# Gate steps, silu and first Down splits in other places around the end of the Up stage

## The chip, the cores and the metric

The kernel runs on one core of one Trainium2 chip. The metric is the device time of one execution in microseconds (us), lower is better. Inside the core, TensorE (PE) multiplies, ScalarE (ACT) and VectorE (DVE) do elementwise work, GpSimd (POOL) does elementwise work and starts some transfers, and SyncE (SP) starts most transfers. Each of them runs its own list of instructions strictly in order, and waits at an instruction until what it needs is there.

## The reference

One decoder layer: a conditioned norm, a mixer (linear recurrence and sparse attention side by side), a gated residual, and then the part that matters here, a gated MLP with a causal convolution of width 3 and a gate vector `gt2` that is one of six products of the condition `c`:

```python
mod = cs @ w_ada[l] + b_ada[l]
sh1, sc1, gt1, sh2, sc2, gt2 = [m[:, None, :] for m in jnp.split(mod, 6, axis=-1)]
...
h2 = rmsnorm(x, norm2_g[l]) * (1.0 + sc2) + sh2
u = causal_dwconv(h2 @ w_up[l], conv_w[l], conv_b[l])
a, v = jnp.split(u, 2, axis=-1)
x = x + gt2 * ((jax.nn.silu(a) * v) @ w_down[l])
```

There are 512 tokens, a model width of 1024 and an inner width of 2816, all in float32.

## The kernel before

Every large product is made of three: each float32 operand is split into a high part (a CAST on ACT, L150) and a low part (a TENSOR_TENSOR subtraction on DVE, L151), and `mm3` (L154 to L156) multiplies high by high, high by low and low by high into one PSUM bank. So a weight tile must have passed ACT for its first matmul and DVE for the first one that reads its low part. `split` and `mm3` are helpers, so almost all of this work carries lines 150 to 156, and is told apart by tile names.

The stages from the middle of the kernel on are:

- **Up, eight early tiles** (loop at L2062), then **seven groups** (`x_group`, L1985). A group is a block product of Up for one pair of weight columns: PE works through x-products and v-products, while ACT and DVE split the next weights and make the convolution taps of results (`taps`, L1767: one ACT and two DVE instructions, from PSUM into an SBUF tile `y`). `held` is a list of three functions that the group before left for this one to run (taps, silu and gate products).
- **Up, eight tail tiles** (loop at L2085). They are called T0 to T7 below; T0 and T1 are the two halves of one load, and so on. Each is 24 matmuls of 128x512 (`u<-...`), from weights that are split on the way (`piece`, `parts`). Behind the matmuls of a tile the loop runs `up_post` (L1802) for the tile two before it: `post_taps`, then `post_gate`. `gate` (L1775) is a silu on ACT (L1778) for even tiles, and for odd tiles three or four products and sums on POOL (L1785 to L1794).
- **Down**: steps u = 0, 1, ... of 24 matmuls of 128x512 each (`dn<-...`), called D0, D1, ... below. In D0 to D10 each step adds three matmuls to each of eight PSUM accumulators in turn. `dn_load(u)` fetches weights, `dn_split(u)` splits them (two casts on ACT, two subtractions on DVE), and `a_split` splits the left operand (`as<-ga`). `ahead_of(u)` runs `dn_load(u + 3)` and `dn_split(u + 1)` ahead of the matmuls of step u. All eight PSUM banks are in use: the accumulators of D0 take the banks that the taps of T0 to T7 leave, the last of them T7's.

Beside this, `gt2` is made by sixteen **gate steps** (`last_add`, L1507): an ACT instruction scales a fetched row block `aw` of `w_ada` (L1510), POOL adds it to `gt2` (L1511), and SP starts the fetch of the next block (`last_fetch`, L1499). The first eight steps make the left half of `gt2`, the other eight the right half. Then `last_split` splits a half into `rhi` and `rlo`, and `last_spread` (L1522) sums it over the partitions with two matmuls and copies the result back with ACT (L1526).

`EARLY` (L54) says for how many Down steps the left operand is split already in the tail of Up; `put_by` (L1809) does one such split for each `beside()` there, and also stores tiles that are needed much later to DRAM (`later<-gb`). `back` (L1831) fetches them again. Temporary 128x512 tiles (`y`, `aw`, `rhi`, `rlo`) share a ring of eight buffers, so a fetch into such a tile waits for the last reader of the tile that lay there.

The order of the work is the order in which the code is written: no scheduler moves instructions.

Of the kernel before, what the change touches and what calls it, by code (L numbers as in the profile page):

```python
# [50 lines left out]
EPOS = 1  # L51
VLAG = 1
ADL = 1
EARLY = 6  # L54
PRE = 4
NU = NFF // 2
XS = (2, 3, 4, 5, 6, 7, 8)
# [52 lines left out]
def hybrid_layer_kernel(ctx: ExitStack, tc: tile.TileContext, d: dict, out: bass.AP, dbg=None):  # L110
# [21 lines left out]
    def PS(s="ps"):  # L132
        return psum.tile([P, 512], F32, tag="b", name=nm(s))
# [1373 lines left out]
    def last_add(s, res):  # L1507
        r, q, k = last_raw.pop(0)
        acc = res[:, q * 512:(q + 1) * 512]
        sc.activation(r, r, AF.Copy, scale=cs[:, k:k + 1])  # L1510
        gp.tensor_tensor(acc, acc, r, ALU.add)  # L1511
        last_fetch(s)

    last_parts = []
# [4 lines left out]
        split(hi, lo, res[:, q * 512:(q + 1) * 512])  # L1519
        last_parts.extend((hi, lo))  # L1520

    def last_spread(res, q):  # L1522
        ps = PS()
        for n in range(2):
            pe.matmul(ps, onesr, last_parts.pop(0), start=(n == 0), stop=(n == 1))
        sc.copy(res[:, q * 512:(q + 1) * 512], ps)  # L1526


    x1 = []
# [272 lines left out]
    def up_post(st):  # L1802
        post_taps(st)
        post_gate(st)
# [4 lines left out]
    def put_by(now):  # L1809
        for j in sorted(full_at, key=full_at.get):  # L1810
            if now >= full_at[j] + 4:
                del full_at[j]
                sp.dma_start(later[j], PB.pop(j)[:, 0:3])
                if place[j] < EARLY:
                    unsplit.append(j)
        if unsplit and XT < now:
            j = unsplit.pop(0)
            a_split(place[j], PA.pop(j))

# [139 lines left out]
    def prepare_plain(n):  # L1959
        p = prep[n]  # L1960
        p["b"] = [G([2, 4, P], F32R, s="wg") for _ in range(2)]
        split(*p["b"], p["raw"][:, 0].rearrange("p (b k) f -> p b k f", b=2))
# [22 lines left out]
    def x_group(n):  # L1985
# [13 lines left out]
        sc.copy(m1, X)  # L1999
        v_mm(V[0], p["v1"], range(4))  # L2000
        held.pop(0)()
        if n > 4:
            last_add(5, gt2)
        beside()
        x_mm(X, half(p["t12"], 1), ops[2], False)
        x_mm(Z, half(p["t12"], 0), ops[1])
# [16 lines left out]
        ve.tensor_tensor(R, n5, X, ALU.subtract)  # L2023
        if more:
            prepare_plain(n + 1)
        v_mm(V[1], p["v2"], range(4))
        taps(uf[1], 0, j + NU)
        last_add(5, gt2)
# [1 line left out]
        v_mm(V[1], p["v2"], range(4, KT))  # L2030
        if more:
            prepare_rest(n + 1)
        x_mm(X, p["x4"], h22, False)
        if more:
            prepare_other(n + 1)
        else:
            piece()
            last_fetch(5)
        del prep[n]

        def first():
# [43 lines left out]
    for st in range(NH, nst):  # L2085
        beside()
        if st == nst - 3:
            dn_load(0)
        elif st == nst - 1:
            dn_load(1)  # L2090
        up_mm(st, full)
        if held:
            for f in held:
                f()
            held.clear()
        elif st > NH + 1:
            up_post(st - 2)
        for _ in range(2 if st == NH else st < NH + 6):
            last_add(5, gt2)
        if st in (NH + 2, nst - 1):  # L2100
            last_spread(gt2, st == nst - 1)
        if st in (NH + 1, nst - 2):
            last_split(gt2, st == nst - 2)
    dn_split(0)
    up_post(nst - 2)
    up_post(nst - 1)
    dn_load(2)
    n = 2 * NU

    def ahead_of(u):  # L2110
        if u + 3 < n:
            dn_load(u + 3)
        if u == 0:
            put_by(tick[0] + 9)
            assert not full_at and not unsplit
        if u + 1 < n:
            dn_split(u + 1)

    for u in range(NU - 1):
        ahead_of(u)  # L2120
        if 0 <= u - EARLY + 1 < PRE:
            back(PAIRS[u - EARLY + 1])
        if 0 <= u - EARLY < PRE:
            a_split(u - EARLY + NU, PB.pop(PAIRS[u - EARLY]))
        for m in TERMS[0]:
            for i in range(2):
                dn_mm(u, m, i)
# [118 lines left out]
```

## Time and profile before

| what | value |
|---|---|
| time, median of 3 runs | 681.27 us (681.12 to 681.4) |
| time of the profiled execution | 680.94 us |
| its span, first to last instruction | 679.2 us |
| mean granted TensorE clock | 0.999 of full speed |
| busy time of PE / DVE / ACT / POOL | 662.6 / 549.6 / 382.7 / 179.4 us |
| the groups, by the PE's records | about 370 to 516.4 us |
| T0 to T7 | 516.4 to 562.7 us |
| D0 onward | from 565.0 us |

A time in a row of the profile is counted from the start of the span. A row of the timeline gives start, duration, engine, line, operation and tiles, and in brackets how long the engine had been idle before and which engine and line ended that. The waits view sums such idle times by who waited for whom. Matmuls overlap each other: one of 128x512 is recorded as 0.39 us, but in steady work the next one starts 0.23 us after it. A gap between starts therefore shows a loss better than the idle time does.

### The profile page before, as it was taken

The page shows a single profiled execution, that of the slowest core. Times are in us where ns is not written, and L with a number is a line of the kernel's source. Part 1 is how long each engine was busy: PE and PEld are TensorE (multiplying, and loading weights), DVE is VectorE, ACT ScalarE, POOL GpSimd, SP SyncE. Part 2 cuts the span into 40 slices and gives each one's busy share as a digit, 9 for nine tenths or more (in the row PEclk, how much of TensorE's full clock was granted, in tenths as well). Part 3 has the DMA queues.
Part 4 walks back from the last instruction along what each step waited for, and adds up shares of the span by engine and source line. Part 5 has one row for each costly group of instructions (what it writes and reads, how often), then busy time and mean ns, then how long its engine had stood idle before and what let it go on. Part 6 is the DMA issues. An engine that isn't in the chain of part 4 may idle for free. (4 is left out here: it accounts for less than half of the span.)

```text
span 679.2 us, 11713 instructions
## 1 busy us (share of the span) xinstructions
PE 662.6 (98%) x4400; PEld 557.9 (82%) x4400; DVE 549.6 (81%) x1038; ACT 382.7 (56%) x713; POOL 179.4 (26%) x172
## 2 busy tenths in 40 slices
PE   8999999999999999999999999999999997999996
PEld 4778898788888888888988989889898785888885
DVE  5788988979899878688778778898876877676997
ACT  5756437747677777246465536455465646464451
POOL 1006121000010100100456444465555874100000
PEclk9999999999999999999999999999999999999999
DMA  9936363566213316036668699999987782896672
GB/s 332 412 143 208 95 213 124 190 216 219 80 48 114 106 58 249 10 125 192 195 165 250 164 282 223 242 264 305 240 235 209 204 289 61 304 362 218 216 280 93
DMA packets 101885, 134.67 MB, mean 198 GB/s; under 512 B 6507, under 2 KB 67780, under 8 KB 101829
## 3 DMA queue, kind: packets, MB, share of 16 engines
q1 hardware_dynamic: 96885, 121.28, 52.8%
q0 software_dynamic: 4512, 11.54, 9.9%
q10 hardware_dynamic: 432, 1.12, 0.4%
q8 instruction: 34, 0.56, 0.3%
q14 instruction: 22, 0.18, 0.1%
HBM read 125.39 MB, written 31.60 MB: 231 GB/s over the span
## 5 line engine op out<-in xcount | busy, mean ns | idle before, releaser
L151 DVE TENSOR_TENSOR wlo<-raw,whi 128x1024 fp32r<-128x1024 f32 (+1 forms) x53 | 69.5, 1312 | 37.1 <-ACT whi L150 37.1
L156 PE MATMUL u<-h2h,wlo 128*128 128x512 f32 (+1 forms) x248 | 93.5, 377 | 1.5 <-DVE wlo L151 1.5
L154 PE MATMUL u<-h2h,whi 128*128 128x512 f32 (+1 forms) x248 | 93.5, 377 | 0.0
L155 PE MATMUL u<-h2l,whi 128*128 128x512 f32 (+1 forms) x248 | 93.4, 377 | 0.0
L150 ACT CAST whi<-raw 128x1024 fp32r<-128x1024 f32 (+1 forms) x53 | 53.9, 1019 | 18.2 <-PE u L155 7.9
L156 PEld LDWEIGHTS u<-h2h,wlo 128*128 128x128 f32 x248 | 46.7, 188 | 11.2 <-DVE wlo L151 2.7
L154 PEld LDWEIGHTS u<-h2h,whi 128*128 128x128 f32 x248 | 46.8, 189 | 7.7
L155 PEld LDWEIGHTS u<-h2l,whi 128*128 128x128 f32 x248 | 46.8, 189 | 7.6
L150 ACT CAST whi<-wd 128x1024 fp32r<-128x1024 f32 x20 | 21.1, 1055 | 39.6 <-PE dn L156 32.0
L372 POOL TENSOR_TENSOR hrs<-hrs,mhalf 128x4 f32<-128x4 f32 (+2 forms) x16 | 18.6, 1172 | 90.7 <-DVE hrs L371 88.6
L1087 ACT ACTIVATE pt<-pt,mx 128x128 f32<-128x128 f32 (+3 forms) x64 | 35.9, 564 | 9.2 <-DVE mx L1071 8.2
L154 PE MATMUL pT<-hT,whi 128*128 128x512 f32 x96 | 38.4, 400 | 0.0
L151 DVE TENSOR_TENSOR wlo<-wd,whi 128x1024 fp32r<-128x1024 f32 x20 | 25.5, 1276 | 15.2 <-ACT whi L150 15.2
L155 PE MATMUL pT<-hT,whi 128*128 128x512 f32 x96 | 37.5, 391 | 0.0
L156 PE MATMUL pT<-hT,wlo 128*128 128x512 f32 x96 | 37.5, 391 | 0.0
L154 PE MATMUL dn<-whi,as 128*128 128x512 f32 x88 | 34.4, 391 | 1.6 <-ACT whi L150 1.6
L155 PE MATMUL dn<-wlo,as 128*128 128x512 f32 x88 | 34.6, 393 | 1.3 <-DVE wlo L151 1.1
L156 PE MATMUL dn<-whi,as 128*128 128x512 f32 x88 | 34.3, 389 | 0.0
L1127 ACT COPY pT<-F 128x512 f32<-128x512 f32 (+2 forms) x52 | 25.8, 499 | 13.2 <-PE F L1120 13.2
L1071 DVE CUSTOM_DVE_ANT_0 pt<-S,cmask 128x128 f32<-128x128 f32 (+3 forms) x64 | 29.7, 486 | 2.1 <-PE S L1067 2.0
L1792 POOL TENSOR_TENSOR ga<-y,y 128x256 f32<-128x256 f32 x11 | 13.7, 1243 | 60.5 <-ACT y L1778 49.2
L1511 POOL TENSOR_TENSOR gt<-gt,aw 128x512 f32<-128x512 f32 x16 | 23.8, 1486 | 21.8 <-ACT aw L1510 21.5
(409 smaller groups left out, 2022.7 us busy)
## 6 DMA issues: line engine op xcount, KB each, us to landing
raw<-in_w_up SPq DMA_DIRECT2D x44, 512.0 KB, 6.4
aw<-in_w_ada SPq DMA_DIRECT2D x24, 512.0 KB, 3.9
ada<-in_ada_first SPq DMA_DIRECT2D x16, 512.0 KB, 8.1
raw<-in_w_in SPq DMA_DIRECT2D x7, 1024.0 KB, 5.0
wt<-in_w_down POOLq DMA_DIRECT2D x11, 512.0 KB, 9.0
wd<-in_w_down SPq DMA_DIRECT2D x11, 512.0 KB, 3.8
wt<-in_w_down SPq DMA_DIRECT2D x10, 512.0 KB, 9.7
wt<-in_w_down POOLq DMA_DIRECT2D x5, 1024.0 KB, 10.2
```

Source lines behind the costliest of these rows:

```text
L150: sc.copy(hi, src)
L151: (eng or ve).tensor_tensor(lo, src, f32(hi), ALU.subtract)
L154: pe.matmul(o, ah, bh, start=start, stop=False, skip_group_check=True)
L155: pe.matmul(o, ah, bl, start=False, stop=False, skip_group_check=True)
L156: pe.matmul(o, al, bh, start=False, stop=stop, skip_group_check=True)
L372: gp.tensor_tensor(o, o, mhalf[:, 0:n], ALU.pow)
L1071: ve.tensor_tensor_reduce(pt[:, e * W:(e + 1) * W], ps[:, e * W:(e + 1) * W], cmask[:, 512 - W:512], -1.0, 1e30, ALU.add, ALU.min, mx[:, e ...
L1087: sc.activation(pt[:, sl], pt[:, sl], AF.Exp, bias=mx[:, e:e + 1], scale=-1.0, accum_out=su[:, h % 2, e:e + 1])
L1127: sc.copy(pT, ps[:, 0:n * P])
L1511: gp.tensor_tensor(acc, acc, r, ALU.add)
L1792: gp.tensor_tensor(a[:, 0], g[:, 0:256], y[:, 0:256], ALU.mult)
```

## The change

- All sixteen gate steps run inside the groups. Before, the first five groups had one each, the last two groups two each, and the tail seven. Now every group has two, and the last has two more.
- `last_spread` is cut in two: the two matmuls stand ahead of T2 and ahead of T4, the copy (`last_out`) follows behind the tile's other work. Before, matmuls and copy came together behind T2 and behind T7. The splits of the two halves are made behind T1 and T3.
- In the tail, the gate of a tile runs one tile later than its taps (`post_gate(st - 3)`, `post_taps(st - 2)`); the gates of the last two tiles run in D0.
- Four left operands are split early, not six, and one for every other tile. `back` and the splits of the second phase that hang on `EARLY` come two steps earlier.
- `dn_split(1)` stands ahead of the taps of T7, and `put_by` for the rest in D1 and not in D0.
- T0's weights go to tiles of the large pool (`wg`) in place of the pair `whi`, `wlo`.

```diff
-EARLY = 6
+EARLY = 4
@@ last_spread
-    def last_spread(res, q):
-        ps = PS()
+    last_ps = []
+
+    def last_spread():
+        last_ps.append(PS())
         for n in range(2):
-            pe.matmul(ps, onesr, last_parts.pop(0), start=(n == 0), stop=(n == 1))
-        sc.copy(res[:, q * 512:(q + 1) * 512], ps)
+            pe.matmul(last_ps[0], onesr, last_parts.pop(0), start=(n == 0), stop=(n == 1))
+
+    def last_out(res, q):
+        sc.copy(res[:, q * 512:(q + 1) * 512], last_ps.pop())
@@ put_by
-        if unsplit and XT < now:
+        if unsplit and XT < now and (now - XT) % 2:
@@ x_group
         held.pop(0)()
-        if n > 4:
-            last_add(5, gt2)
+        last_add(5, gt2)
         beside()
...
         if more:
             prepare_plain(n + 1)
+        else:
+            last_add(5, gt2)
         v_mm(V[1], p["v2"], range(4))
         taps(uf[1], 0, j + NU)
         last_add(5, gt2)
...
         if more:
             prepare_rest(n + 1)
+        else:
+            last_add(5, gt2)
         x_mm(X, p["x4"], h22, False)
         if more:
             prepare_other(n + 1)
         else:
-            piece()
-            last_fetch(5)
+            piece(True)
@@ the tail
+        if st in (NH + 2, NH + 4):
+            last_spread()
         up_mm(st, full)
...
         elif st > NH + 1:
-            up_post(st - 2)
-        for _ in range(2 if st == NH else st < NH + 6):
-            last_add(5, gt2)
-        if st in (NH + 2, nst - 1):
-            last_spread(gt2, st == nst - 1)
-        if st in (NH + 1, nst - 2):
-            last_split(gt2, st == nst - 2)
+            if st > NH + 2:
+                post_gate(st - 3)
+            post_taps(st - 2)
+        if st in (NH + 1, NH + 3):
+            last_split(gt2, st == NH + 3)
+        if st in (NH + 2, NH + 4):
+            last_out(gt2, st == NH + 4)
     dn_split(0)
-    up_post(nst - 2)
-    up_post(nst - 1)
+    post_gate(nst - 3)
+    post_taps(nst - 2)
     dn_load(2)
+    dn_split(1)
+    post_taps(nst - 1)
@@ ahead_of
-        if u == 0:
+        if u == 1:
             put_by(tick[0] + 9)
             assert not full_at and not unsplit
-        if u + 1 < n:
+        if 0 < u < n - 1:
             dn_split(u + 1)
 
     for u in range(NU - 1):
         ahead_of(u)
+        if u == 0:
+            post_gate(nst - 2)
+            post_gate(nst - 1)
```

The next lists show what that does to the instruction lists. A row has line, operation, written tile, read tiles and size; lines of the changed kernel are a few higher (L1774 for L1770, L1782 for L1778, L1530 for L1526).

The first place is ACT's list at the end of the last group, from the taps of the group's result (`y<-uf`) to the casts of T0's and T1's weights. Before:

```order
L1770 ACTIVATE y_5957<-uf_5796,cv 128x512
L1510 ACTIVATE aw_5853<-aw_5853,cs 128x512
L150 CAST whi_5994<-raw_5786 128x1024
L150 CAST whi_6001<-raw_5786 128x1024
L1770 ACTIVATE y_6030<-u_5798,cv 128x512
L1778 ACTIVATE y_5957<-y_5957 128x512
```

The same place on ACT in the changed kernel:

```order
L1510 ACTIVATE aw_5873<-aw_5873,cs 128x512
L1774 ACTIVATE y_5981<-uf_5816,cv 128x512
L1510 ACTIVATE aw_5967<-aw_5967,cs 128x512
L1510 ACTIVATE aw_5987<-aw_5987,cs 128x512
L150 CAST wg_6020<-raw_5806 128x1024
L150 CAST whi_6025<-raw_5806 128x1024
```

Three gate steps (`aw`) stand there and not one, two of them between the taps and the cast for T0, which now writes `wg`.

The second place is ACT's list in the tail around the cast of T4's weights (`whi_6159` before, `whi_6162` now). Before, behind the silu of T0:

```order
L1778 ACTIVATE y_6137<-y_6137 128x512
L1510 ACTIVATE aw_6055<-aw_6055,cs 128x512
L1526 COPY gt_3810<-ps_6146 128x512
L150 CAST as_6151<-ga_4798 128x1024
L150 CAST whi_6159<-raw_6065 128x1024
```

In the changed kernel, from the cast of T3's weights (`whi_6120`) on:

```order
L150 CAST whi_6120<-raw_6017 128x1024
L1774 ACTIVATE y_6148<-u_6024,cv 128x512
L1530 COPY gt_3810<-ps_6116 128x512
L150 CAST as_6154<-ga_4490 128x1024
L150 CAST whi_6162<-raw_6081 128x1024
L1782 ACTIVATE y_6148<-y_6148 128x512
```

The silu of T0 went from ahead of T4's cast to behind it, and no gate step is left there.

The third place is the start of Down, first on ACT: `whi_6374` and `wg_6378` before, `whi_6361` and `wg_6365` now, are D0's weights, the next such pair D1's. Before:

```order
L150 CAST rhi_6327<-gt_3810 128x512
L1770 ACTIVATE y_6361<-u_6250,cv 128x512
L1526 COPY gt_3810<-ps_6370 128x512
L150 CAST whi_6374<-raw_6246 128x1024
L150 CAST wg_6378<-raw_6246 128x1024
L1770 ACTIVATE y_6382<-u_6293,cv 128x512
L1778 ACTIVATE y_6382<-y_6382 128x512
L1770 ACTIVATE y_6387<-u_6336,cv 128x512
L150 CAST whi_6407<-raw_6332 128x1024
```

On ACT in the changed kernel, at the same place:

```order
L1774 ACTIVATE y_6357<-u_6251,cv 128x512
L150 CAST whi_6361<-raw_6247 128x1024
L150 CAST wg_6365<-raw_6247 128x1024
L1774 ACTIVATE y_6374<-u_6285,cv 128x512
L150 CAST whi_6383<-raw_6327 128x1024
L150 CAST wg_6387<-raw_6327 128x1024
L1774 ACTIVATE y_6391<-u_6331,cv 128x512
L1782 ACTIVATE y_6374<-y_6374 128x512
```

The split and the copy of `gt2` are gone from here, and D1's casts stand ahead of the taps of T7 (`y_6387` before, `y_6391` now). DVE's list in the changed kernel, from the low part of D0's second pair of weights on, shows the same:

```order
L151 TENSOR_TENSOR wg_6366<-raw_6247,wg_6365 128x1024
L1775 SCALAR_TENSOR_TENSOR y_6374<-u_6285,cv,y_6374 128x511
L1776 SCALAR_TENSOR_TENSOR y_6374<-u_6285,cv,y_6374 128x510
L151 TENSOR_TENSOR wlo_6384<-raw_6327,whi_6383 128x1024
L151 TENSOR_TENSOR wg_6388<-raw_6327,wg_6387 128x1024
L1775 SCALAR_TENSOR_TENSOR y_6391<-u_6331,cv,y_6391 128x511
L1776 SCALAR_TENSOR_TENSOR y_6391<-u_6331,cv,y_6391 128x510
```

Before, the two low parts of D1 stood behind the taps of T7; now the taps of T7 stand behind them.

## The prediction

> **What bounds the kernel now.** The page puts PE at 98% of the span, and the granted clock at full speed, so time can only go where PE stands still. I first asked the waits view for PE from 340 us on, where Up and Down lie:
>
> ```profile
> PE dn L154 <- ACT whi L150: 1.6, 1, 1.6
> PE u L156 <- DVE wlo L151: 1.5, 2, 1.2
> PE dn L155 <- DVE wlo L151: 1.1, 1, 1.1
> PE dn L154 <- DVE y L1772: 0.8, 1, 0.8
> ```
>
> There are five waits in all, for split weights (`whi`, `wlo`) and once for taps (`y`). The timeline of PE then shows where they are:
>
> ```profile
> 516.61 0.40 PE L155 MATMUL u<-h2l,whi 128*128 128x512 f32 x1
> 517.32 0.50 PE L156 MATMUL u<-h2h,wlo 128*128 128x512 f32 x1 [0.32 <-DVE wlo L151]
> 517.65 0.39 PE L154 MATMUL u<-h2h,whi 128*128 128x512 f32 x1
> ...
> 528.11 0.39 PE L155 MATMUL u<-h2l,whi 128*128 128x512 f32 x1
> 528.47 0.50 PE L156 MATMUL u<-h2h,wlo 128*128 128x512 f32 x1
> ...
> 539.74 0.39 PE L155 MATMUL u<-h2l,whi 128*128 128x512 f32 x1
> 541.29 0.50 PE L156 MATMUL u<-h2h,wlo 128*128 128x512 f32 x1 [1.16 <-DVE wlo L151]
> ...
> 562.75 0.39 PE L1525 MATMUL ps<-rhi,onesr 128*128 128x512 f32 x1
> 562.98 0.40 PE L1525 MATMUL ps<-rlo,onesr 128*128 128x512 f32 x1
> 564.99 0.49 PE L154 MATMUL dn<-whi,as 128*128 128x512 f32 x1 [1.62 <-ACT whi L150]
> 566.62 0.50 PE L155 MATMUL dn<-wlo,as 128*128 128x512 f32 x1 [1.14 <-DVE wlo L151]
> ...
> 571.06 0.39 PE L156 MATMUL dn<-wg,as 128*128 128x512 f32 x1
> 572.26 0.47 PE L154 MATMUL dn<-wg,as 128*128 128x512 f32 x1 [0.81 <-DVE y L1772]
> ```
>
> In steady work starts lie 0.23 us apart (562.75 to 562.98). What is over that is lost: 0.48 in T0, 0.13 in T2, 1.32 in T4, 1.78 and 1.40 at the first two matmuls of D0, and 0.97 at D0's last accumulator, in sum 6.1 us. Behind a wait the next start comes 0.33 and not 0.23 later (517.32 to 517.65), five times 0.1, so **6.6 us** are lost. From 380 us to T0, and from D1 to the last product, no other wait of note shows. This is the most that the change can win here, since it leaves PE's work as it is.
>
> Why PE waits there is read from ACT and DVE:
>
> ```profile
> 534.46 0.63 ACT L1778 ACTIVATE y<-y 128x512 f32<-128x512 f32 x1 [4.88 <-DVE y L1772]
> ...
> 537.03 1.05 ACT L150 CAST whi<-raw 128x1024 fp32r<-128x1024 f32 x1
> ...
> 558.28 0.63 ACT L1778 ACTIVATE y<-y 128x512 f32<-128x512 f32 x1 [4.26 <-DVE y L1772]
> ...
> 563.41 0.58 ACT L1526 COPY gt<-ps 128x512 f32<-128x512 f32 x1 [1.85 <-PE ps L1525]
> 563.89 1.05 ACT L150 CAST whi<-raw 128x1024 fp32r<-128x1024 f32 x1
> 564.84 1.05 ACT L150 CAST wg<-raw 128x1024 fp32r<-128x1024 f32 x1
> 565.79 0.78 ACT L1770 ACTIVATE y<-u,cv 128x512 f32<-128x512 f32 x1
> ...
> 569.78 0.76 ACT L1770 ACTIVATE y<-u,cv 128x512 f32<-128x512 f32 x1
> ```
>
> ```profile
> 538.92 2.31 DVE L151 TENSOR_TENSOR wlo<-raw,whi 128x1024 fp32r<-128x1024 f32 x1
> ...
> 564.97 1.60 DVE L151 TENSOR_TENSOR wlo<-raw,whi 128x1024 fp32r<-128x1024 f32 x1 [1.84 <-ACT whi L150]
> 566.49 1.21 DVE L151 TENSOR_TENSOR wg<-raw,wg 128x1024 fp32r<-128x1024 f32 x1
> 567.63 0.74 DVE L1771 SCALAR_TENSOR_TENSOR y<-u,cv,y 128x511 f32<-128x511 f32 x1
> 568.40 0.75 DVE L1772 SCALAR_TENSOR_TENSOR y<-u,cv,y 128x510 f32<-128x510 f32 x1
> ```
>
> ACT stands at a silu for 4.88 us, then does a gate step, a copy and an early split, and only at 537.03 casts T4's weights; DVE's part ends at 541.23, and PE goes on at 541.29. At Down it stands at the copy of `gt2` until PE has made the second spread (563.0), and only then casts D0's weights, which nobody needed to wait for.
>
> **The change part by part.** PE's list has the same matmuls. Without a wait it would run T0 and T1 from 516.38 (0.23 ahead of 516.61), 24 times 0.227 = 5.45 us each, to 527.29, the first spread (0.46) and T2 and T3 to 538.66, the second spread and T4 to T7 to 560.93. I set each engine's new list against these times.
>
> *D0's first matmuls (1.78 + 1.40 and a restart, 3.3 us).* The copy waits for a spread that now stands ahead of T4, 22 us earlier. ACT casts D0's weights when the buffers of T6 come free, at 555.5; with the 1.05 of a cast, and 0.95 from cast to cast, DVE has both low parts by about 559 (1.05 + 1.2 + 1.2, from the rows at 563.89 to 566.49), even 560.5 if each takes 0.4 to 1.1 more. PE needs the first at 561.2. The term goes to nothing; what is late next there is the transfer of D0's weights, whose place in SP's list hardly moves.
>
> *T4 (1.4 us).* Its cast no longer stands behind the silu. It waits for T2's end (533.2), the cast and the subtraction end by 535.5, by 536.7 if DVE takes 2.31 again, and PE wants it at 539.5. Goes to nothing. T3, T5, T6 and T7 are laid out alike: two tiles of buffer, so 5.45 us for 2.3 us of splitting. The two spreads need `rlo` at 527.5 and 538.9; on ACT and DVE it ends near 526.8 and 537.8, with less than a microsecond to spare. I keep 0.2 us for that.
>
> *D0's last accumulator (0.97 and a restart).* This stays. T7's taps, at 569.78 on ACT before, now follow D1's two casts and two subtractions. Before, from ACT's cast at 563.89 through two subtractions to the end of the next taps at 569.15 was 5.26 us, with 0.38 of delay in it (1.60 against 1.21). The same run begins at T7's end, 560.93, and PE needs the bank 21 matmuls later, 4.77 us. So 0.3 to 0.7 is lost, with a restart, and up to 2.4 us if DVE comes late out of the tail: it has fourteen instructions, some 12.7 us, between T5's end (550.0) plus a cast and the bank. I take **0.6**.
>
> *T0 (0.6 us).* T0's cast is free of PE now, but two gate steps stand ahead of it. These rows are of ACT's and SP's timeline, of the tile view of `aw` from 470 to 565 us, and of the transfer engines from 502 to 516 us (forty slices, busy tenths):
>
> ```profile
> 512.13 0.71 ACT L1510 ACTIVATE aw<-aw,cs 128x512 f32<-128x512 f32 x1
> 507.96 0.34 SPq L1499 DMA_DIRECT2D aw<-in_w_ada  x1
> DMA to landing us min/median/max: 5.3/7.9/9.4
> DMA  9998999999999999973387610028789999999999
> ```
>
> The step at 512.13 stays, a second follows, then cast and subtraction: 512.13 + 2 x 0.71 + 1.05 + 1.22 = 515.8, ahead of 516.84, when PE reads the low part. So T0 gains its 0.6 if the last fetch is there. This is a new wait: behind the gate step stand the casts of T0 and T1 and the taps. The buffer of that fetch comes free with the same POOL product as that of the SP row, so it is asked for at 507.96, and must land within 4.9 us, by 512.84. Fetches of `aw` landed in 5.3 to 9.4, but the transfer engines stand empty near 510.5, so the fetch that before was asked for at the very same moment had landed in 2.5. I take it as in time.
>
> *The groups.* Five of them get one more ACT step of 0.71 and one more addition on POOL of 1.3. The last two groups had both already, at the same place, and PE lost nothing there. One row of the waits from 380 to 515 us, and one of the windows (busy time of PE, PE's loads, DVE, ACT and POOL in a group's 21 us):
>
> ```profile
> ACT u L2007 <- PE uf L156: 15.5, 6, 2.8
> 435.00:456.00 21.00, 21.00 (x132) 18.95 (x131) 17.86 (x22) 10.70 (x16) 11.25 (x10) 1.00 0.95 256
> ```
>
> ACT waits 2.6 us a group for PE right behind that place, so the step lies in idle time; DVE is busy for 17.86 of the 21 us of a group. Cost zero; less than nothing it can't be, since PE loses nothing there; for more, see the rivals. The seven steps that leave the tail (ACT 0.71, POOL 1.3 each) free those engines where PE waited. Moving the splits of D4 and D5 into Down costs DVE 1.2 us in a step of 5.45 that has 2.5 to 3.7 us of work, which PE covers. `put_by` in D1 lets the loads of D4 go ahead of a store that waits for POOL: also no cost.
>
> Sum: 6.6 lost before, 0.2 + 0.6 after, **5.8 us less**: 680.94 becomes 675.1. The median of the runs is 0.33 above the profiled one, so **675.4 us**.
>
> **The rivals.** *The last fetch comes late* (chance 0.10). If it takes the 7.9 of its kind it lands at 515.9, ACT's cast waits behind it, and T0's low part is there at 518.8, 2.0 us late: 677.4; with 9.4 it is 678.9. The empty slices speak against it.
>
> *DVE's backlog moves the wait to D0's last accumulator* (0.06): 2.4 in place of 0.6, 677.2. For it speaks that POOL works beside DVE in the tail too.
>
> *POOL against DVE in the groups* (0.05):
>
> ```profile
> L151 DVE TENSOR_TENSOR wlo<-raw,whi 128x1024 fp32r<-128x1024 f32 x14 | 17.1, 1223 | 20.9 <-ACT whi L150 20.9
> L151 DVE TENSOR_TENSOR wlo<-raw,whi 128x1024 fp32r<-128x1024 f32 x6 | 11.7, 1947 | 0.0
> ```
>
> A low part took 1.22 us from 380 to 520 us and 1.95 from 520 to 560, where POOL has its seven additions. Five more in the groups could each hold up one subtraction by 1.1 (2.31 against 1.22); if all lay on PE's path that gives back 5.5 us: 680.9, no change. Against it: DVE would still be busy for 19 of 21 us, and the last two groups show no such wait. The Trainium skill, in "SBUF — State Buffer", section "Who interferes with whom", says that a DVE instruction with two SBUF inputs and a GpSimd instruction that reads SBUF block each other for a whole instruction; by that rule alone the additions only change their place, and what they cost depends on who waits. The trace agrees in sign: 1.95 against 1.22.
>
> *The change doesn't do what it says* (0.03): some wait that I count as gone is set by something that stays; no change.
>
> *Slower* (0.06): the extra fetch in each group comes late and holds ACT, with the cast of the next weights behind it.
>
> ```profile
> 487.17 0.33 SPq L1499 DMA_DIRECT2D aw<-in_w_ada  x1
> 499.68 0.72 ACT L1510 ACTIVATE aw<-aw,cs 128x512 f32<-128x512 f32 x1
> ```
>
> It was asked for 12.5 us ahead of its use. In five groups the 5.8 us are gone when each loses 1.2, so when it lands 13.7 us or more after its issue; at 14.2 it would be 5 x 1.7 = 8.5, 683.9 in all. The longest landing of `aw` was 9.4, but the transfer engines are 95% busy there.
>
> **How the numbers follow.** The forecast, with T0, T4 and D0's start cured, has 0.70. Of the others 0.10 and 0.06 are faster too, 0.08 make no change and 0.06 are slower. A measurement can tell 0.2% (1.4 us) from no change, so faster has 0.86, the same 0.08, slower 0.06. The range goes from 674.6 (nothing but 0.3 left at D0) to 678.2, which takes in the backlog and most of the late fetch.
>
> **What would show it.** In the changed trace D0 should start near 561 without a wait, with one short gap 21 matmuls later for `y`; T4 should have no gap; T0 none, unless ACT stands at a gate step near 512.8 for a transfer. ACT should have two gate steps in every group and PE no gap before 516. It is wrong if PE shows gaps in the groups, if a spread waits for `rlo` by over 1 us, or if D4 to D7 wait for weights.

## The result, and the profile after

The changed kernel takes **675.81 us** (median of 6 runs, 675.61 to 675.97) against 681.27 us (680.9 to 681.9, 6 runs). The ratio is 0.9919, with a 95% interval of 0.9906 to 0.9932, so it is faster by 0.8%. The forecast was 675.4, in a range of 674.6 to 678.2. The profiled execution took 675.84 us with a span of 674.0 us, against 680.94 and 679.2.

The waits view of PE from 340 us on has one line left, where there were five waits before:

```profile
PE ps L1527 <- DVE rlo L151: 1.0, 1, 1.0
```

The timeline of PE shows the five places at which the prediction looked: T0, the first spread and T2, the second spread and T4, D0's start, and D0's last accumulator.

```profile
516.42 0.40 PE L154 MATMUL u<-h2h,wg 128*128 128x512 f32 x1
516.65 0.40 PE L155 MATMUL u<-h2l,wg 128*128 128x512 f32 x1
516.88 0.39 PE L156 MATMUL u<-h2h,wg 128*128 128x512 f32 x1
...
527.32 0.40 PE L1527 MATMUL ps<-rhi,onesr 128*128 128x512 f32 x1
528.74 0.50 PE L1527 MATMUL ps<-rlo,onesr 128*128 128x512 f32 x1 [1.02 <-DVE rlo L151]
529.08 0.40 PE L154 MATMUL u<-h2h,whi 128*128 128x512 f32 x1
...
540.02 0.39 PE L1527 MATMUL ps<-rhi,onesr 128*128 128x512 f32 x1
540.25 0.39 PE L1527 MATMUL ps<-rlo,onesr 128*128 128x512 f32 x1
540.48 0.40 PE L154 MATMUL u<-h2h,whi 128*128 128x512 f32 x1
...
562.03 0.39 PE L156 MATMUL u<-h2h,wlo 128*128 128x512 f32 x1
562.26 0.39 PE L154 MATMUL dn<-whi,as 128*128 128x512 f32 x1
562.48 0.39 PE L155 MATMUL dn<-wlo,as 128*128 128x512 f32 x1
...
566.79 0.39 PE L156 MATMUL dn<-wg,as 128*128 128x512 f32 x1
567.27 0.47 PE L154 MATMUL dn<-wg,as 128*128 128x512 f32 x1
567.58 0.39 PE L155 MATMUL dn<-wg,as 128*128 128x512 f32 x1
```

Starts lie 0.23 us apart wherever nothing is lost. So T0, the second spread, T4 and D0's start cost nothing now. The first spread's second matmul comes 1.42 us after the first and T2 0.34 after that: 1.19 + 0.11 lost. At D0's last accumulator the step is 0.48 (566.79 to 567.27) and the next 0.31: 0.25 + 0.08. In sum 1.63 us are lost between T0 and D0's end, where it was 6.6. The difference, 4.9, is most of the 5.2 by which the span shrank.

The first spread waits for DVE. These are rows of DVE's and POOL's timelines in T1, and the last one is the same operation (`rlo`) at the second spread, where no product is running on POOL when it starts:

```profile
523.68 1.62 DVE L151 TENSOR_TENSOR as<-ga,as 128x1024 fp32r<-128x1024 f32 x1 [1.70 <-ACT as L150]
525.23 1.76 DVE L151 TENSOR_TENSOR wlo<-raw,whi 128x1024 fp32r<-128x1024 f32 x1
526.91 1.77 DVE L151 TENSOR_TENSOR rlo<-gt,rhi 128x512 fp32r<-128x512 f32 x1
...
524.30 1.61 POOL L1798 TENSOR_TENSOR ga<-ga,gb 128x256 f32<-128x256 f32 x1
525.86 2.27 POOL L1789 TENSOR_TENSOR gb<-y,y 128x512 f32<-128x512 f32 x1
...
538.28 0.68 DVE L151 TENSOR_TENSOR rlo<-gt,rhi 128x512 fp32r<-128x512 f32 x1
```

An early split, T2's low part and `rlo` stand one behind the other, and `rlo` takes 1.77 us in place of 0.68. It ends at 528.68, and PE goes on at 528.74.

Whether the groups paid for the gate steps is read from their window. This row is of before and the one below it of the changed kernel (busy time of PE, PE's loads, DVE, ACT and POOL):

```profile
380.00:516.00 136.00, 136.00 (x846) 122.60 (x845) 111.06 (x133) 70.24 (x103) 71.52 (x64) 1.00 0.94 250
```

```profile
380.00:516.00 136.00, 136.00 (x846) 122.55 (x845) 113.50 (x134) 74.82 (x111) 79.20 (x71) 1.00 0.97 259
```

POOL is busy for 7.7 us more, ACT for 4.6 and DVE for 2.4 (1.5 of it is T0's low part, which now falls into the window), and PE for all of the 136 us in both. The records of matmuls overlap, so a full window alone would not show small gaps, and the starts settle it. This is the start of the same product in the second group and of T0's first one, first before and then in the changed kernel:

```profile
382.26 0.40 PE L154 MATMUL u<-h2h,whi 128*128 128x512 f32 x1
...
516.38 0.40 PE L154 MATMUL u<-h2h,whi 128*128 128x512 f32 x1
```

```profile
382.27 0.40 PE L154 MATMUL u<-h2h,whi 128*128 128x512 f32 x1
...
516.42 0.40 PE L154 MATMUL u<-h2h,wg 128*128 128x512 f32 x1
```

It is 134.12 us before and 134.15 now: the groups cost nothing that can be read.

### The profile page after: what moved, and what is told of

Same layout as the page of the kernel before. It is cut to its first block, busy times and chain, and to the rows that moved or that the text cites. A ratio compares the mean times of both kernels' runs of the same rounds, so it can differ in the third digit from the quotient of the medians.

```text
span 674.0 us, 11718 instructions
## 1 busy us (share of the span) xinstructions
PE 661.5 (98%) x4400; PEld 558.2 (83%) x4400; DVE 547.5 (81%) x1038; ACT 382.7 (57%) x713; POOL 177.5 (26%) x172
## 4 chain that ended last, share of the span: by engine, by line
PE 82%; DVE 10%; ACT 5%; issue 1%; DMA 1%; ACTq 0%; DVEq 0%
PE u L154 8%; PE u L155 8%; PE u L156 8%; PE dn L154 5%; PE dn L156 5%; PE dn L155 5%; PE uf L156 4%; PE uf L155 3%; PE uf L154 3%; PE accq L680 3%; PE oh L154 2%; PE oh L156 2%; PE oh L155 2%; PE oT L1149 2%; PE F L1120 2%; PE pT L154 2%
## 5 line engine op out<-in xcount | busy, mean ns | idle before, releaser
L151 DVE TENSOR_TENSOR wlo<-raw,whi 128x1024 fp32r<-128x1024 f32 (+1 forms) x52 | 66.3, 1277 | 43.3 <-ACT whi L150 43.2
L154 PE MATMUL u<-h2h,whi 128*128 128x512 f32 (+1 forms) x240 | 90.4, 377 | 0.0
L155 PE MATMUL u<-h2l,whi 128*128 128x512 f32 (+1 forms) x240 | 90.2, 376 | 0.0
L156 PE MATMUL u<-h2h,wlo 128*128 128x512 f32 (+1 forms) x240 | 90.0, 375 | 0.0
L156 PEld LDWEIGHTS u<-h2h,wlo 128*128 128x128 f32 x240 | 45.2, 188 | 8.3
L154 PEld LDWEIGHTS u<-h2h,whi 128*128 128x128 f32 x240 | 45.3, 189 | 7.5
L155 PEld LDWEIGHTS u<-h2l,whi 128*128 128x128 f32 x240 | 45.3, 189 | 7.4
L1774 ACT ACTIVATE y<-uf,cv 128x512 f32<-128x512 f32 x14 | 10.9, 776 | 30.2 <-DVE uf L2026 28.2
```

What stands on the lines that cost most here:

```text
L151: (eng or ve).tensor_tensor(lo, src, f32(hi), ALU.subtract)
L154: pe.matmul(o, ah, bh, start=start, stop=False, skip_group_check=True)
L155: pe.matmul(o, ah, bl, start=False, stop=False, skip_group_check=True)
L156: pe.matmul(o, al, bh, start=False, stop=stop, skip_group_check=True)
```

## The experiments

Kernels whose programs are alike up to T0 reach the first spread anywhere from 526.75 to 527.62 us, so their spans differ by up to 0.9 us for that alone. Spans of one kernel differ from one execution to the next by up to 3.5 us (split_grp, 672.1 to 675.6), and what lies around a span took 1.7 to 4.0 us. So by the ratios only grp_d1 is told from the changed kernel on the better side, and before_early4, spread_end, spread_end_copy_later and gates_tail_silu on the worse. Everything smaller is read from the starts of PE's matmuls in the one profiled execution of each kernel. The table has the profiled span, the median, the ratio to before with its 95% interval, and the time that PE lost at the five places (start to start over 0.23, with the restart behind it).

| kernel | span | median | ratio | T0 | first spread, T2 | second spread, T4 | D0's start | last accumulator |
|---|---|---|---|---|---|---|---|---|
| before | 679.2 | 681.27 | | 0.58 | 0.23 | 1.42 | 3.29 | 1.04 |
| changed | 674.0 | 675.81 | 0.9919 (0.9906 to 0.9932) | 0 | 1.30 | 0 | 0 | 0.33 |
| split_grp | 672.4 | 675.91 | 0.9916 (0.9898 to 0.9935) | 0 | 0 | 0 | 0 | 0.33 |
| split_t0 | 673.0 | 674.96 | 0.9908 (0.9891 to 0.9925) | 0 | 0 | 0 | 0 | 0.33 |
| pool_held | 672.5 | 675.48 | 0.9907 (0.9889 to 0.9925) | 0 | 0 | 0 | 0 | 0.33 |
| grp_d1 | 673.8 | 674.25 | 0.9888 (0.9873 to 0.9903) | 0 | 0 | 0 | 0 | 0 |
| silu_here | 674.2 | 676.26 | 0.9928 (0.9910 to 0.9946) | 0 | 1.31 | 0 | 0 | 0.86 |
| early6 | 673.9 | 677.73 | 0.9930 (0.9913 to 0.9947) | 0 | 1.30 | 0 | 0 | 0.32 |
| before_early4 | 678.3 | 680.10 | 0.9977 (0.9967 to 0.9988) | 0.59 | 0.24 | 0.42 | 2.93 + 1.6 | 0 |
| gates_tail | 673.8 | 676.75 | 0.9927 (0.9912 to 0.9942) | 0 | 0.67 | 0.57 | 0 | 0.32 |
| gates_tail_silu | 681.7 | 683.50 | 1.0033 (1.0019 to 1.0047) | 0 | 0.67 | 6.4 + 2.0 | 0 | 0.33 |
| spread_end | 677.8 | 680.29 | 0.9978 (0.9966 to 0.9990) | 0 | 1.31 | 0 | 2.92 + 1.6 | 0.17 |
| spread_end_copy_later | 677.5 | 679.50 | 0.9966 (0.9950 to 0.9982) | 0 | 1.31 | 0 | 0 | 2.19 + 1.5 |
| t0_old | 674.9 | 677.03 | 0.9937 (0.9922 to 0.9951) | 1.94 | 0.37 | 0 | 0 | 0.32 |

A number behind a plus is what matmuls at half clock behind the stall cost; it is shown with spread_end. In the two gates_tail kernels the second spread stands ahead of T6.

### The first spread: what makes `rlo` late

**split_grp** splits the first half of `gt2` in the last group.

```diff
-        if st in (NH + 1, NH + 3):
-            last_split(gt2, st == NH + 3)
+        if st == NH + 3:
+            last_split(gt2, 1)
@@ x_group, the second gate step of the last group
         else:
             last_add(5, gt2)
+            last_split(gt2, 0)
```

> The changed kernel with one edit: the first half of gt2 is split (rhi, rlo) in the last group instead of in T1. Its eight gate steps are long done there. Theory: the 1.3 us that the changed kernel still loses at the first spread come from VectorE, which in T1 does as, wlo and rlo one behind the other (1.62 + 1.76 + 1.77 us), so that rlo is ready only at 528.7. With rlo out of T1 the spread starts without a wait and T2's low part ends near 527: 1.3 us less, about 674.5 us. Rival 1: the split fits the group as badly as T1, since POOL adds there and VectorE is busy 18 of 21 us; then a new wait in the last group takes back 0.7 to 1.8 us: 675.2 to 676.3. Rival 2: T2's low part is as late as rlo was, and the wait only changes its name: 675.5 to 675.8.

The spread ran without a wait, and no other wait came: PE's waits from 340 us on are an empty list. The span is 1.6 us shorter, 1.3 of it at the spread. By the starts the theory holds, and both rivals fall. The median does not show it: it is 675.91 us, not 674.5, over six executions whose spans go from 672.1 to 675.6.

**split_t0** keeps the work in T1's neighbourhood, but puts it ahead of T1's early split and T2's weights.

```diff
-        if st in (NH + 1, NH + 3):
+        if st in (NH, NH + 3):
```

> The changed kernel with one edit: the first half of gt2 is split at the end of T0's step, so ahead of T1's early split and of T2's weights on ScalarE and VectorE, instead of behind both. The same work in T1, in another order. Theory (it is the sum of VectorE's work in T1 that is late): the spread finds rlo near 525, but T2's low part now ends where rlo ended, near 528.7, while its first reader stands at 528.2: 0.5 us lost there in place of 1.3, so about 675.0 us. Rival (only the place of rlo in the order mattered): no wait at all, 674.5. Second rival (T2's low part is slowed more, beside POOL): the whole 1.3 stays, 675.8.

No wait at all, so the first rival was right here and my theory was not: the order was enough. I had T2's low part end at 528.7; it ended at 527.74 (started 525.98, 1.76 long), 0.8 us ahead of its reader at 528.54. In its new place `rlo` took 0.82 us and not 1.77, because POOL had only just begun.

**pool_held** leaves the lists of ACT and DVE as they are and holds POOL back, with a copy of two columns of `rlo` ahead of its seven gate products.

```diff
+    hold = []
...
+        if hold:
+            hold.append((f, g, y))
+        else:
+            products(f, g, y)
+
+    def products(f, g, y):
         odd, j = divmod(f, NU)
...
         if held:
+            hold.append(None)
             for f in held:
...
             last_split(gt2, st == NH + 3)
+            if st == NH + 1:
+                gp.tensor_copy(res1, last_parts[1][:, 0:2])
+                late_products = hold[1:]
+                hold.clear()
+                for args in late_products:
+                    products(*args)
```

> The changed kernel with POOL's seven gate products of T1 held back: a copy of two columns on POOL, which waits for the first rlo, stands ahead of them. VectorE's list is the same. Theory (VectorE's splits in T1 take 1.62, 1.76 and 1.77 us because POOL works beside them): now they take 1.22, 1.22 and 0.68, rlo ends 2 us sooner, near 526.8, and the first spread starts without a wait: span 672.7 against 674.0. The products follow 3 to 5 us later beside T3's split and taps, which have room. Rival (the splits are slow by themselves, or for another reason): they keep their durations, the spread waits 1 us, span 674.0 or more. Rival 2 (what POOL does later hits the next split): the first spread is free, and a wait of 0.5 us or more comes at T4 or at the second spread.

These are rows of DVE and POOL of this kernel:

```profile
523.53 1.23 DVE L151 TENSOR_TENSOR as<-ga,as 128x1024 fp32r<-128x1024 f32 x1 [1.69 <-ACT as L150]
524.67 1.22 DVE L151 TENSOR_TENSOR wlo<-raw,whi 128x1024 fp32r<-128x1024 f32 x1
525.81 0.69 DVE L151 TENSOR_TENSOR rlo<-gt,rhi 128x512 fp32r<-128x512 f32 x1
...
526.56 0.18 POOL L2121 COPY res<-rlo 128x2 f32<-128x2 f32 x1 [7.92 <-DVE rlo L151]
```

The same three instructions in the same order take 1.23, 1.22 and 0.69 us once POOL stands still, and the spread's 1.3 us are gone. So it is POOL beside DVE that made `rlo` late; with POOL's products where they were, a place of `rlo` ahead of that overlap did as well (split_t0). The products that were held back made nothing late: there is no new wait.

### T4: which part of the change cured it

**silu_here** puts each silu behind its own tile's taps again.

```diff
-            if st > NH + 2:
-                post_gate(st - 3)
             post_taps(st - 2)
+            post_gate(st - 2)
...
     dn_split(0)
-    post_gate(nst - 3)
     post_taps(nst - 2)
```

> The changed kernel with one part undone: in the tail each silu stands directly behind its tile's taps again, not a tile later. Theory of the prediction (T4's cast was late because it stood behind a silu that waits for VectorE): T4's wait of 1.3 us with its restart comes back, about 677.2 us. Rival: the silu was late only because a gate step, the copy and a slow VectorE came together; with the gate steps gone from the tail ScalarE casts T4's weights by 535 even behind the silu, PE wants the low part at 540.7, and nothing comes back: 675.8, at most 676.1.

Rows of ACT, and one of PE:

```profile
531.59 0.63 ACT L1782 ACTIVATE y<-y 128x512 f32<-128x512 f32 x1 [2.88 <-DVE y L1776]
...
534.20 1.05 ACT L150 CAST whi<-raw 128x1024 fp32r<-128x1024 f32 x1 [0.56 <-PE u L155]
...
567.45 0.47 PE L154 MATMUL dn<-wg,as 128*128 128x512 f32 x1 [0.62 <-DVE y L1776]
```

The rival holds. ACT still waits at the silu, but only until 531.59, and T4's cast then waits 0.56 us for PE to leave its buffer: the silu isn't what it stands behind. What the silu a tile later is worth here is 0.5 us at D0's last accumulator (0.86 against 0.33 lost).

**before_early4** is the kernel before with four early splits, in every other tile, and nothing else of the change.

```diff
-EARLY = 6
+EARLY = 4
@@ put_by
-        if unsplit and XT < now:
+        if unsplit and XT < now and (now - XT) % 2:
```

> The kernel before with one part of the change alone: four early splits in place of six, and only in every second tile of the tail. Gate steps, spreads, silus and D1's split stay where they were. Theory (T4 was late because T2 held an early split of 1.05 us on ScalarE and 1.76 on VectorE ahead of the taps that the silu waits for, and T4's own step another): the silu comes near 532.9 and T4's low part by 539.7, so T4's wait of 1.3 us goes; D0's stalls of 3.2 us stay: span 677.9 against 679.2. Rival (silu and gate steps hold the cast whatever the splits): T4 still waits 0.5 us or more, span 678.4 to 679.5. If the first spread is as crowded as in the changed kernel, nothing shows there, since before it stood behind T3's start.

PE and ACT of this kernel:

```profile
539.90 0.39 PE L155 MATMUL u<-h2l,whi 128*128 128x512 f32 x1
540.45 0.50 PE L156 MATMUL u<-h2h,wlo 128*128 128x512 f32 x1 [0.16 <-DVE wlo L151]
...
532.94 0.63 ACT L1778 ACTIVATE y<-y 128x512 f32<-128x512 f32 x1 [3.20 <-DVE y L1772]
```

The silu comes at 532.94, as expected, against 534.46 before, and of the 1.42 us at T4 0.42 are left. So one early split less ahead of T2's taps gives most of T4's gain, with gate steps and silu where they were.

**early6** is the other direction: the changed kernel with six early splits, one in every tile.

```diff
-EARLY = 4
+EARLY = 6
@@ put_by
-        if unsplit and XT < now and (now - XT) % 2:
+        if unsplit and XT < now:
```

> The changed kernel with six early splits again, one in every tile of the tail. Theory (the splits alone made T4 late): T4's wait is back in part, 0.5 to 1.3 us, or the second spread waits for rlo: span 674.6 to 675.4. Rival (with the silu a tile behind and no gate steps ahead, T4's cast has room for one more split): no new wait there, and D0's last accumulator no later than 0.5 us: span 673.8 to 674.4. The first spread keeps its 1.3 us in both.

No wait at T4, so the rival holds: with the silu behind the cast and no gate step ahead of it, two more splits find room.

**gates_tail** moves the gate steps back: one in each of the first five groups, seven in T0 to T5, the second spread ahead of T6.

```diff
         held.pop(0)()
-        last_add(5, gt2)
+        if n > 4:
+            last_add(5, gt2)
@@ x_group, twice
-        else:
-            last_add(5, gt2)
...
             piece(True)
+            last_fetch(5)
@@ the tail
-        if st in (NH + 2, NH + 4):
+        if st in (NH + 2, NH + 6):
             last_spread()
...
+        for _ in range(2 if st == NH else st < NH + 6):
+            last_add(5, gt2)
-        if st in (NH + 1, NH + 3):
-            last_split(gt2, st == NH + 3)
+        if st in (NH + 1, NH + 5):
+            last_split(gt2, st == NH + 5)
-        if st in (NH + 2, NH + 4):
-            last_out(gt2, st == NH + 4)
+        if st in (NH + 2, NH + 6):
+            last_out(gt2, st == NH + 6)
```

> The changed kernel with the gate steps where they were: one a group for the first five groups, and seven in T0 to T5. The second half of gt2 is then split in T5 and spread ahead of T6 (its last step is in T5); silu a tile behind, early splits and D1's split stay. T4 was cured by something else than the silu's place, since silu_here has no wait there. Theory 1 (the gate steps beside VectorE and ahead of the casts made T4 late): with the silu a tile behind there is still a wait of 0.5 to 1.4 us at T4 or T5, span 674.5 to 675.6. Theory 2 (each of the two, the gate steps and the silu, was enough to be rid of it): no wait at T4, span 673.8 to 674.3. If the five additions in the groups cost something (rival: POOL against VectorE), the groups get shorter here: T0 starts before 516.0 counted from the same first group.

T4 has no wait. From the start of the same product in the second group (382.16 here, 382.27 in the changed kernel) to T0 (516.33 and 516.42) it is 134.17 and 134.15 us: the five additional steps in the groups cost nothing that can be read. The two spreads lose 0.67 and 0.57 us, together 1.24 where the changed kernel loses 1.30. With the silu moved, the gate steps' move brings nothing that can be read.

**gates_tail_silu** adds the edit of silu_here to it.

> As gates_tail, and the silu stands directly behind its taps again. Theory 2 (each of the two was enough): only now T4's wait of about 1.2 us with its restart is back, span 675.3 to 676.5. Theory 1: the wait is as in gates_tail, the two spans lie within 0.5. Rival (it was the copy of the first spread behind the silu, which has not moved, or the six early splits, of which two are gone): no wait at T4 in either.

The rival holds at T4: there is no wait in either kernel, with silu and gate steps back and four early splits. A new wait, which no theory had, stands at the second spread, as rows of POOL and ACT show:

```profile
550.17 1.26 POOL L1789 TENSOR_TENSOR gb<-y,y 128x512 f32<-128x512 f32 x1 [3.80 <-DVE y L1776]
...
553.79 1.26 POOL L1511 TENSOR_TENSOR gt<-gt,aw 128x512 f32<-128x512 f32 x1
...
555.08 0.62 ACT L150 CAST rhi<-gt 128x512 fp32r<-128x512 f32 x1 [6.98 <-POOL gt L1511]
```

The last addition to `gt2` stands on POOL behind gate products that wait for taps of the same tile; ACT waits for the addition with the cast of `rhi`, and T6's weights stand behind that. Together the two undone parts cost more than all that the change won (ratio 1.0033), with the second spread kept early: the kernel before, which has both but spreads behind T7, has no such wait.

### D0's start and T0

**spread_end** makes the second spread behind T7 again, with its copy.

```diff
-        if st in (NH + 2, NH + 4):
+        if st == NH + 2:
             last_spread()
...
-        if st in (NH + 2, NH + 4):
-            last_out(gt2, st == NH + 4)
+        if st == NH + 2:
+            last_out(gt2, 0)
+        if st == nst - 1:
+            last_spread()
+            last_out(gt2, 1)
```

> The changed kernel with one part undone: the second spread and its copy stand behind T7 again (its split stays in T3). Theory: ScalarE stands at the copy until PE has made the spread, and D0's casts stand behind it: D0 starts 1.8 us late and its second matmul 1.4 us, with the restart 3.3 us: about 679.1 us. Rival: what delayed D0 before was VectorE's backlog from the gate steps and the silus in the tail; with these gone D0 is late by less than 1 us: below 676.8.

Rows of PE, and two of the windows (the number behind POOL's is the granted clock):

```profile
563.41 0.49 PE L154 MATMUL dn<-whi,as 128*128 128x512 f32 x1 [1.62 <-ACT whi L150]
564.67 0.50 PE L155 MATMUL dn<-wlo,as 128*128 128x512 f32 x1 [0.77 <-DVE wlo L151]
...
566.13 0.63 PE L154 MATMUL dn<-whi,as 128*128 128x512 f32 x1
566.56 0.63 PE L155 MATMUL dn<-wlo,as 128*128 128x512 f32 x1
...
561.00:565.00 4.00, 1.62 (x6) 0.80 (x5) 1.61 (x2) 3.17 (x5) 0.00 (x0) 1.00 0.90 344
566.00:569.00 3.00, 3.00 (x8) 2.32 (x8) 2.96 (x4) 2.13 (x4) 0.00 (x0) 0.50 0.01 5
```

The theory's wait is back: 1.78, 1.03 and a restart, 2.9 us. And behind it the clock fell to half: matmuls start 0.43 us apart from 565.7 to 569.1, which costs another 1.6.

**spread_end_copy_later** leaves the spread there and puts only the copy behind D0's casts.

```diff
+        if st == nst - 1:
+            last_spread()
     dn_split(0)
+    last_out(gt2, 1)
```

> The changed kernel with the second spread behind T7 again, as in spread_end, but with its copy behind the two casts of D0. Theory (only the copy's place in ScalarE's list held D0 up; the spread itself may stand anywhere): D0 starts without a wait, profiled span 674.0 as in the changed kernel (673.7 to 674.4), 3.8 less than spread_end's 677.8. Rival (the early place of the spread matters too, since its rlo or its bank comes late at T7): a wait of 1 us or more at the spread or at D0, span 675 or more.

ACT and PE:

```profile
562.43 0.59 ACT L1530 COPY gt<-ps 128x512 f32<-128x512 f32 x1 [4.12 <-PE ps L1527]
562.91 0.79 ACT L1774 ACTIVATE y<-u,cv 128x512 f32<-128x512 f32 x1
...
569.13 0.47 PE L154 MATMUL dn<-wg,as 128*128 128x512 f32 x1 [1.95 <-DVE y L1776]
```

D0 starts without a wait, so it was the copy's place that held it there. But ACT stood at the copy for 4.12 us all the same, and now the taps of T6, D1's casts and the taps of T7 stand behind it: the wait went to D0's last accumulator, 2.2 us, with 1.5 at half clock behind it. Each theory had half of it; of the places tried, only a spread ahead of T4 or T6 lets the copy through without holding up Down.

**t0_old** takes the pair `whi`, `wlo` for T0 again.

```diff
-            piece(True)
+            piece()
```

> The changed kernel with T0's weights in the pair whi, wlo again, so that their cast must wait for PE to leave that buffer. Theory of the prediction (the cast was bound to PE): T0's third matmul waits for wlo again, 0.5 us and a restart, span about 674.6 against 674.0. Rival (before, it was the one gate step ahead of the cast that made it late; two of them now hide the buffer's wait, or make it worse): 0.7 more than that, span 675.3. Second rival: no wait, 674.0.

ACT and PE:

```profile
514.81 1.05 ACT L150 CAST whi<-raw 128x1024 fp32r<-128x1024 f32 x1 [1.44 <-PE u L155]
...
518.58 0.50 PE L156 MATMUL u<-h2h,wlo 128*128 128x512 f32 x1 [1.68 <-DVE wlo L151]
```

The cast waits for PE until 514.81, as it did in the kernel before (514.96). New is that the last of POOL's additions, from 515.86 on, runs beside its subtraction: the low parts of T0 and T1, from 515.90 on, took 3.76 us together, where before they took 1.23 and 1.22. T0 loses 1.94, more than the 0.58 of before, so with two gate steps ahead of T0 the other buffer is needed. The rival had the size, but not the reason: by these rows it isn't the steps on ACT that are late, it is the addition that follows them. The first spread, that much later, loses 0.37 in place of 1.30, and the span is 0.9 longer.

### A kernel that beats both

**grp_d1** is split_grp with D1's splits behind T7's taps.

```diff
-    dn_split(1)
     post_taps(nst - 1)
+    dn_split(1)
```

> The changed kernel with two edits: the first half of gt2 split in the last group (as in split_grp, span 672.4 without a wait), and D1's two splits behind T7's taps instead of ahead of them. Theory: T7's taps end near 563 and free the bank well ahead of D0's last accumulator, whose 0.33 us go; D1's low parts end near 565.5, and D1 needs them from 566: span 672.1. Rival (D1's weights, now behind the taps, come late): a wait of 0.3 to 1.5 us at D1, span 672.4 to 673.6.

PE around D0's last accumulator, and a window near the program's start:

```profile
566.96 0.39 PE L156 MATMUL dn<-wg,as 128*128 128x512 f32 x1
567.18 0.39 PE L154 MATMUL dn<-wg,as 128*128 128x512 f32 x1
...
10.00:15.00 5.00, 4.35 (x29) 2.21 (x27) 2.91 (x8) 1.95 (x6) 1.32 (x3) 0.69 1.03 408
```

Nothing is lost from T0 into D1: all of the theory. This profiled execution had a stretch of lower clock at 10 to 20 us, where the programs are alike, and its span is no measure of the edit. The median is 674.25 us, ratio 0.9888 (0.9873 to 0.9903), against 0.9919 (0.9906 to 0.9932) for the changed kernel: some 2 us better. By PE's starts 1.63 us of that are accounted for, 1.30 at the first spread and 0.33 by D1's split. So D1's split ahead of T7's taps, a part of the change, is better undone, though only by a third of a microsecond.

## Why the prediction was right, and where it was not

The median came out 0.4 us above the forecast, inside the range. By PE's starts the change won 4.9 us and not 5.8, since 1.6 us stayed where 0.8 was forecast: 1.1 more at the spreads, 0.3 less at D0's last accumulator. The median shows 5.5 won; the part of it that the starts do not explain brought it closer to the forecast than the working was, and that is luck. By its steps:

- *D0's start (3.3 us to nothing).* Right, and for the reason given: with the late copy 2.9 us came back (spread_end), and it was the copy and not the spread (spread_end_copy_later). D0 starts at 562.26, not near 561, because the first spread pushed everything back by 1.3.
- *T4 (1.4 us to nothing).* The size was right, and the reason incomplete. The prediction put it to the silu's place. silu_here shows no wait with the silu in its old place. Much of what made the silu so late was the early split in T2, and taking that away alone gives 1.0 of the 1.4 (before_early4); in gates_tail_silu, where silu and gate steps are in their old places and the rest of the change stands, no wait is left at T4. With the silu moved and the gate steps gone the splits could all have stayed (early6). So, with the rest of the change, either way is enough; the prediction did not see that the change did the same thing twice.
- *T0 (0.6 us).* Right: the fetch came in time, and the gate steps ran at 512.19 without a wait. That the buffer is what makes it possible is shown by t0_old. It was closer than forecast: the low part started at 514.50 beside POOL's additions, took 2.04 us where the sum had 1.22, and ended at 516.54, not at 515.8, only 0.34 ahead of its reader at 516.88.
- *The two spreads (0.2 us).* This is the term that failed: 1.30 us at the first, nothing at the second. The prediction had `rlo` end near 526.8 and kept 0.2 us for being late. That end is what DVE's undisturbed durations give from the 523.68 at which the chain did start (1.22 + 1.22 + 0.68). It ended at 528.68. pool_held shows the missing 2 us as POOL's work beside three DVE instructions. The rows of before had shown it, `wlo` at 1.95 us on average between 520 and 560; I had weighed it in the groups, as a rival, and not at this place, where it decided. The prediction named a wait of over 1 us for `rlo` as what would make it wrong, and there was one of 1.02. The total came close because nothing else went wrong by as much.
- *D0's last accumulator (0.6 us).* 0.33, at the lower end of 0.3 to 0.7: DVE came out of the tail on time, and the two subtractions took 1.22 us each.
- *The groups (nothing).* Right: PE has no new gap, and gates_tail reaches T0 no sooner.

Of the rivals, the late fetch, the late group fetch and the backlog at D0's last accumulator did not come. POOL against DVE came, but around T0 and in T1 and not in the groups. The Trainium skill says in "SBUF — State Buffer", section "Who interferes with whom", that a DVE instruction with two SBUF inputs contends with a GpSimd instruction that reads SBUF. pool_held agrees: 1.62, 1.76 and 1.77 us became 1.23, 1.22 and 0.69 when POOL stood still.

What stays open: the parts were undone one at a time (D1's split only together with an earlier `rlo`) and in one pair, not in every combination, so how much of T4's wait the gate steps made isn't known by itself. In gates_tail the silu ahead of T1's early split, and with it the chain to `rlo`, comes 1.55 us sooner than in the changed kernel (520.53 against 522.08): the low parts of T0 and T1 take 1.49 and 1.23 us there, and 2.04 and 2.31 beside the further additions of the last group. Whether moving those additions alone would free the first spread was not tried.

## What to carry to other kernels

Before the last instruction of a chain is put close to its reader, its duration is to be taken from rows with the same neighbours on the other engines, not from its fastest row. On an in-order engine an instruction that waits for a late result can be moved, but then it stops whatever stands behind it in the new place; only making the result early frees the engine. Where a change cures one wait in two ways, undo them one at a time: one may be kept for nothing. And a part that cures no wait, like D1's split here, may cost something.

## What the runs showed of the hardware that was not expected

**DVE's splits and POOL's products take turns, so what a split loses depends on the product that is running when it starts.** `rlo` (128x512) took 0.68 us alone, 1.22 at 528.34 in the kernel before, and 1.77 in the changed one; a low part of 128x1024 took 1.22, 1.76 or 2.31 (other values, such as 1.62 and 2.04, occur). A POOL product of 128x256 takes 0.74 us alone, one of 128x512 1.26 (550.17 in gates_tail_silu). Beside the first a split lost up to about 0.54, beside the second up to about 1.1, whatever its own length, so a short one suffers most for its size. A split that starts first loses nothing and the product waits, as at the second spread: `rlo` at 538.28 takes 0.68, and the product that starts at 538.50 takes 1.06 in place of 0.74. The Trainium skill, in "SBUF — State Buffer", section "SBUF: two separate sides", has the one that starts first hold the shared ports for its whole instruction, and the other blocked. The rows of T1 above agree: the product of 524.30 starts inside the split of `as` and takes 1.61, `wlo` starts inside that product and loses 0.54, the next product starts inside `wlo` and takes 2.27, and `rlo` starts inside that one and ends 0.55 behind it.

**A stall of PE has a price behind it.** In four kernels (spread_end, spread_end_copy_later, before_early4, gates_tail_silu) the granted clock fell to 0.50 for some 3 to 6 us behind a stall of 2 to 5 us, which cost 1.5 to 2 us more. In the profiled execution of the kernel before, with nearly the same stall at D0 (1.78 and 1.40 lost), it did not fall, nor behind the 1.84 of t0_old. The Trainium skill, in "TensorE: Matmul & The Clock Gate", section "Part 1: The HAM clock gate", has the clock halve after an idle window of about 3.4 us that runs freely; here 1.95 us of idle PE (spread_end_copy_later) were enough. A free-running window would fit that nearly the same stall is paid for in one execution and not in another, but no run here shows it. So the change may also have taken away a cost that the profile of before did not show.
